# A first stage of v in two passes, with the shift's share of half 0 added later by a matvec

## The chip, the cores and the metric

The kernel runs on one core of a Trainium2 chip. The metric is the device time of one execution in microseconds. It is one launch; everything from the first load to the last store is in it.

## The reference, cut to what matters

One layer of a diffusion backbone over 640 tokens (128 context tokens, 512 sample tokens), model width 2048, all in float32. The part that the change touches is the beginning:

```python
sh1, sc1, g1, sh2, sc2, g2 = modulation(cond, w_mod, b_mod)   # silu(cond) @ w_mod + b_mod, 2 conditions
u = rmsnorm(x, g_pre_mix) * (1.0 + sc1) + sh1
q, k, v, o, ig, fg, z, xbc, dt = split(u @ w_in)              # v: 1024 columns, gates: 48 columns
```

After it come a bidirectional mLSTM with four heads (it uses q, k, v and the gates ig, fg), a bidirectional SSD (it uses xbc after a small convolution, and dt), the output projection, and an MLP. A row of u can be written as x·a1 times the norm of its token plus the shift, where a1 = g_pre_mix (1 + sc1). So a column block of u @ w_in is the norm of the token times (x·a1) @ w_in plus sh1 @ w_in; the last term is one row for each of the two conditions.

## The kernel before, in words

Activations lie with the model dimension on the partitions (KT = 16 slices of 128 rows, `xT`, `ah`, `al`) and the 640 tokens in the free dimension; NT = 5 token tiles of 128. A product of the first stages is made three times in fp32r: each operand is split into a high part and a rest, and hi·hi, hi·lo and lo·hi are accumulated. `split_block` loads one packed weight block of 128x1024 (512 KB) into a `raw` buffer, copies it to `whi` on ACT (L202) and subtracts into `wlo` on DVE (L203). `mm_b` (L231 to L233) makes three matmuls with 512 moving columns for one token tile and one slice; `mm_a` (L215) makes six with 384 or 256 moving columns, weights stationary.

The first stage (the loop over k from L292 on) does this. All of x is loaded; the sum of squares over the 16 slices is made on ACT (L298) and DVE (L300), and `norm_row` (L165, L176) turns it into one factor per token, spread over the partitions, `rb`. `mod1(k)` loads four blocks of `w_mod` (as two transfers of 1024 KB into `m1`, 4 buffers), multiplies them with the conditions in 16 small matmuls of 256 columns whose stationary tile is 128x32 (L319), and gets the scale `a1` and the shift `modT` of slice k by way of a copy, two transposes (L256) and a sum (`sm`, L257). Then u = x·a1·rb (L339), `ah` = u + shift (L340), `al` = the rest (L341). Slice k is multiplied into two banks for the gates (`gps`), and each pair of slices into five banks for half 0 of v (`vps`). Every slice needs its scale and its shift before it can be multiplied.

After the stage: the gates are transposed, and a long chain of small operations on DVE and ACT (L402 to L525) makes the decay factors from them. Half 1 of v is a projection of its own (`proj_b("v", 1)`), then come q and k of head 0, `mlstm(0)`, q and k of head 1, and so on; the convolution tiles 8 and 12 (`conv_tile`) stand ahead of `mlstm(3)`. Each projection takes `mod_step`s along, 96 and later 128 in all, which load one block (`mraw`) and make the rest of the modulation with four small matmuls (L267). PSUM has 8 banks: in the first stage 5 `v`, 2 `g`, 1 `s`; afterwards 5 `mm`, 2 `ms`, 1 `tr`. The tile `fm` (128x640) has 6 buffers for q, k, convolution tiles and short-lived work.

The framework orders the instructions of each engine and of the load queue on SP ahead of time, from its own model of the times; loads are issued in that order as soon as their buffer is free.

## Time and profile before

| | us |
|---|---|
| median of 3 runs (range) | 2903.09 (2900.97 to 2903.12) |
| the profiled execution | 2905.62 |
| its span, first to last instruction | 2903.6 |
| mean granted TensorE clock | 0.995 of full speed |
| TensorE (PE) busy | 2830.6 |

A busy time counts an instruction from its start to its modelled end; the matmuls of a stream overlap, so their pace is read from the starts in the timeline and not from the mean length. An idle time is put down to the wait that ended last.

### The profile page before, as it was taken

How to read it: one execution, taken by the hardware profiler on the slowest of the kernel's cores; microseconds unless marked ns; L12 is line 12 of the kernel's file. 1: busy time of each engine (PE TensorE's matmuls, PEld its weight loads, DVE VectorE, ACT ScalarE, POOL GpSimd, SP SyncE). 2: the span in 40 equal slices, each digit the busy share in tenths (PEclk: the TensorE clock that was granted, in tenths of full speed). 3: DMA queues.
4: the chain of work that ended last, by engine and by line, in shares of the span. 5: the costliest groups of instructions: out<-in, count | busy, mean ns of one | idle time of the engine just before them, and what ended most of it. 6: DMA issues, size and time to landing. Idle time of an engine off the chain costs nothing.

```text
span 2903.6 us, 48371 instructions
## 1 busy us (share of the span) xinstructions
PE 2830.6 (97%) x18868; PEld 2629.6 (91%) x18868; DVE 1945.6 (67%) x3102; ACT 1280.8 (44%) x2307; POOL 439.4 (15%) x466
## 2 busy tenths in 40 slices
PE   6999999999999999999999999999999999999996
PEld 4679997887887888999999999999999999999996
DVE  4463474786756745677777666666776677678977
ACT  3322333334423433554444444444555555555363
POOL 0000000223211000000000000000014444543212
PEclk9999999999999999999999999999999999999998
DMA  9743434545647767555444333333458999897253
GB/s 369 283 138 115 138 128 138 174 160 159 211 140 227 251 229 263 174 182 167 154 158 143 115 113 109 112 111 117 141 146 169 211 211 204 188 203 180 88 207 142
DMA packets 211748, 498.52 MB, mean 172 GB/s; under 512 B 22424, under 2 KB 111768, under 8 KB 211008
## 3 DMA queue, kind: packets, MB, share of 16 engines
q1 hardware_dynamic: 153872, 429.38, 44.3%
q0 software_dynamic: 39792, 45.73, 10.0%
q10 hardware_dynamic: 17856, 20.32, 1.9%
q8 instruction: 148, 2.42, 0.3%
q14 instruction: 80, 0.66, 0.1%
HBM read 405.33 MB, written 44.97 MB: 155 GB/s over the span
## 4 chain that ended last, share of the span: by engine, by line
PE 83%; DVE 6%; DMA 4%; issue 3%; ACT 1%; POOL 1%; ACTq 0%; DVEq 0%; SPq 0%; POOLq 0%
PE mm L810 17%; PE mm L808 17%; PE mm L809 17%; PE mm L215 11%; PE mm L231 3%; PE mm L233 3%; PE mm L232 3%; PE tr L267 3%; DMA raw<-in_w 2%; DVE wlo L936 2%; POOL pc L1217 1%; PE mod L319 1%; PE vps L231 1%; PE vps L232 1%; DMA R<-hd 1%
## 5 line engine op out<-in xcount | busy, mean ns | idle before, releaser
L936 ACT CAST whi<-raw 128x512 fp32r<-128x512 f32 (+1 forms) x659 | 499.0, 766 | 558.3 <-PE mm L809 323.6
L936 DVE TENSOR_TENSOR wlo<-raw,whi 128x512 fp32r<-128x512 f32 (+1 forms) x659 | 578.2, 886 | 240.2 <-ACT whi L936 234.9
L810 PE MATMUL mm<-ah,wlo 128*128 128x320 f32 x1536 | 475.2, 311 | 5.2 <-DVE wlo L936 4.9
L808 PE MATMUL mm<-ah,whi 128*128 128x320 f32 x1536 | 478.4, 312 | 1.2 <-ACT whi L936 1.2
L809 PE MATMUL mm<-al,whi 128*128 128x320 f32 x1536 | 476.2, 310 | 0.0
L202 ACT CAST whi<-raw 128x1024 fp32r<-128x1024 f32 x162 | 169.3, 1047 | 419.1 <-PE mm L233 131.0
L810 PEld LDWEIGHTS mm<-ah,wlo 128*128 128x128 f32 x1536 | 288.1, 188 | 11.5 <-DVE wlo L936 6.3
L1217 POOL DMA_DIRECT2D pc<-ev x275 | 241.2, 905 | 366.3 <-ACT ev L1216 356.1
L808 PEld LDWEIGHTS mm<-ah,whi 128*128 128x128 f32 x1536 | 288.6, 188 | 8.4 <-issue 6.2
L203 DVE TENSOR_TENSOR wlo<-raw,whi 128x1024 fp32r<-128x1024 f32 x162 | 201.8, 1248 | 140.7 <-ACT whi L202 138.6
L809 PEld LDWEIGHTS mm<-al,whi 128*128 128x128 f32 x1536 | 288.7, 188 | 5.5 <-issue 4.9
L215 PE MATMUL mm<-ah,whi 128*128 128x256 f32 (+1 forms) x768 | 189.6, 319 | 0.0
L215 PE MATMUL mm<-al,whi 128*128 128x256 f32 (+1 forms) x768 | 188.8, 318 | 0.0
L215 PE MATMUL mm<-ah,wlo 128*128 128x384 f32 (+1 forms) x768 | 185.8, 316 | 0.0
L231 PE MATMUL mm<-whi,ah 128*128 128x512 f32 x400 | 161.6, 404 | 0.0
L232 PE MATMUL mm<-wlo,ah 128*128 128x512 f32 x400 | 160.0, 400 | 0.0
L233 PE MATMUL mm<-whi,al 128*128 128x512 f32 x400 | 159.4, 399 | 0.0
L808 PE MATMUL mm<-q,whi 128*128 128x320 f32 x512 | 158.0, 309 | 0.0
L810 PE MATMUL mm<-q,wlo 128*128 128x320 f32 x512 | 157.9, 308 | 0.0
L1216 ACT COPY ev<-mm 128x320 f32<-128x320 f32 x275 | 115.9, 425 | 69.7 <-DMA pc<-ev 45.4
L215 PEld LDWEIGHTS mm<-ah,whi 128*128 128x128 f32 x768 | 121.0, 188 | 10.2 <-issue 9.1
L215 PEld LDWEIGHTS mm<-ah,wlo 128*128 128x128 f32 x768 | 120.6, 188 | 6.9 <-issue 5.8
(399 smaller groups left out, 6709.0 us busy)
## 6 DMA issues: line engine op xcount, KB each, us to landing
raw<-in_w SPq DMA_DIRECT2D x460, 512.0 KB, 3.7
mraw<-in_w SPq DMA_DIRECT2D x128, 512.0 KB, 4.2
pc<-ev POOLq DMA_DIRECT2D x275, 160.0 KB, 5.0
m<-in_w SPq DMA_DIRECT2D x32, 1024.0 KB, 6.8
R<-hd SPq DMA_DIRECT2D x32, 640.0 KB, 6.3
xs<-csd SPq DMA_DIRECT2D x40, 256.0 KB, 5.0
hd<-s ACTq DMA_DIRECT2D x62, 160.0 KB, 3.3
hd<-u ACTq DMA_DIRECT2D x62, 160.0 KB, 1.9
```

Source lines behind the costliest of these rows:

```text
L202: S.copy(hi, t)
L203: V.tensor_sub(lo, t, hi)
L215: PE.matmul(ps[h][:, 0:HW[h]], lhsT=w[:, cs_], rhs=a[:, k, HS[h]], start=(k == 0 and i == 0), stop=(k == KT - 1 and i == 2))
L231: PE.matmul(ps[:, :], lhsT=ah[:, k, tok], rhs=hi[:, wc], start=first, stop=False)
L232: PE.matmul(ps[:, :], lhsT=ah[:, k, tok], rhs=lo[:, wc], start=False, stop=False)
L233: PE.matmul(ps[:, :], lhsT=al[:, k, tok], rhs=hi[:, wc], start=False, stop=last)
L808: PE.matmul(ps, lhsT=wh[:, c], rhs=bh[:, k, :], start=(start and k == 0), stop=False)
L809: PE.matmul(ps, lhsT=wh[:, c], rhs=bl[:, k, :], start=False, stop=False)
L810: PE.matmul(ps, lhsT=wl[:, c], rhs=bh[:, k, :], start=False, stop=(stop and k == nk - 1))
L936: newest[:] = S.copy(hi, src), V.tensor_sub(lo, src, hi)
L1216: S.copy(ev, ps)
L1217: G.dma_start(pi[:, j, :], ev, accum_op=OP.add)
```

## The change

- The stage is cut into two passes over the eight pairs p of slices. In pass 0 `mod1(0, p)` makes the scales of two slices at once; `ah` is x·a1 alone, without norm and without shift, and half 0 of v is multiplied from it. The sums of squares are made along the way, x is loaded pair by pair. At the end of the pass the norm of each token is worked out (`rc5`) and half 0 is multiplied by it as it leaves PSUM. In pass 1 `mod1(1, p)` makes the shifts; u, `ah` and `al` are made as before, and half 1 of v is multiplied in the same stage.
- The blocks of `mod1` come as single transfers of 512 KB, into 5 `m1` and the 2 `mraw` buffers (7 blocks; before, 4 buffers of two blocks).
- The gates become a projection of their own after the stage (`proj_a("g", 0)`).
- The shift's part of half 0 (`v0_steps`): the eight blocks of half 0 are loaded again, multiplied with the shifts in 16 small matmuls of 512 columns, summed over partitions by two full ones, and added to the finished half. These steps take the place of the first eight `mod_step`s (`side_step`).
- `proj_b` takes 12 side steps instead of 8. The convolution tiles 8 and 12 move ahead of `mlstm(0)`, so their two `fm` buffers are held through all heads. The half-0 tile of v is allocated from the start.

```diff
-    for k in range(KT):
-        keys += [("m1", k, j) for j in range(4)]
-        if k % 8 == 0:
-            keys.append(("A", "g", 0, k // 8))
-        if k % 2 == 1:
-            keys.append(("B", "v", 0, k // 2))
-    keys += [("B", "v", 1, j) for j in range(8)]
+    for v in range(2):
+        for p in range(KT // 2):
+            keys += [("m1", v, p, j) for j in range(4)]
+            keys.append(("B", "v", v, p))
+    keys += [("A", "g", 0, j) for j in range(2)]
...
+                for _ in range(2 - j % 2):
+                    side_step()
...
+        def side_step():
+            if first:
+                if next(first[0], "end") == "end":
+                    first.pop()
+                else:
+                    return
+            if mod["n"] < MODCAP[0]:
+                mod_step()
...
-            for k in range(KT):
-                if k % 2 == 0:
-                    SY.dma_start(xT[:, k:k + 2, :], A["xT"][:, k * T:(k + 2) * T].rearrange("p (a b) -> p a b", b=T))
-                sq = rb if k == 0 else (wb, wp)[k % 2].tile([P, 1024], F32, tag=("raw", "mraw")[k % 2], name="sq", bufs=2)[:, 0:T]
-                S.activation(sq, xT[:, k, :], AF.Square)
-                if k:
-                    V.tensor_add(rb, rb, sq)
-            for h in range(2):
-                V.tensor_copy(rb[:, HS[h]], norm_row(rb[:, HS[h]], D,
-                                                     lambda: pv.tile([P, 512], F32, tag="g", name="nrm", bufs=2)))
...
+            def load_m1(v, p):
                 r = []
-                for jj in range(2):
-                    w = p0.tile([P, 2, 1024], F32, tag="m1", name="m1", bufs=4)
-                    b0 = BLK["m1", k, 2 * jj]
-                    SY.dma_start(w, A["w"][b0:b0 + 2].rearrange("b p c -> p b c"))
+                for j in range(4):
+                    i = more["m1"] = more.get("m1", -1) + 1
+                    if i % 7 < 2:
+                        w = wp.tile([P, 1024], F32, tag="mraw", name="mraw", bufs=2)
+                    else:
+                        w = p0.tile([P, 1024], F32, tag="m1", name="m1", bufs=5)
+                    SY.dma_start(w, A["w"][BLK["m1", v, p, j]])
                     r.append(w)
...
-            def mod1(k):
-                ws = load_m1(k)
+            def mod1(v, p):
+                ws = load_m1(v, p)
                 ps = pv.tile([P, 512], F32, tag="s", name="mod1", bufs=1)
                 for kk in range(KT):
                     g = kk % 4
                     PE.matmul(ps[32 * g:32 * g + 32, 0:256], lhsT=scT[:, kk, :],
-                              rhs=ws[kk // 8][:, kk // 4 % 2, g * 256:(g + 1) * 256],
+                              rhs=ws[kk // 4][:, g * 256:(g + 1) * 256],
...
+                for i in range(2):
+                    k = 2 * p + i
+                    if v == 0:
+                        V.tensor_scalar(a1[:, k, :], sm[:, i, :], b1[:, k:k + 1], pp("gpre")[:, k:k + 1],
+                                        OP.add, OP.mult)
+                    else:
+                        V.tensor_scalar(modT[:, k, :], sm[:, i, :], pp("bmod")[:, k:k + 1], None, OP.add)
...
+            def v_pair(vps, v, p):
+                vw = split_block(("B", "v", v, p))
+                for kk in range(2):
+                    k = 2 * p + kk
+                    for t in range(NT):
+                        mm_b(vps[t], t, k, vw[0], vw[1], kk, k == 0, k == KT - 1)
...
-            for k in range(1):
-                mod1(k)
-            for k in range(KT):
-                if k + 1 < KT:
-                    mod1(k + 1)
-                u = p0.tile([P, T], F32, tag="u", name="u", bufs=1)
-                for ci, cc in enumerate((slice(0, P), slice(P, T))):
-                    V.scalar_tensor_tensor(u[:, cc], xT[:, k, cc], a1[:, k, ci:ci + 1], rb[:, cc], OP.mult, OP.mult)
-                    S.activation(ah[:, k, cc], u[:, cc], AF.Identity, bias=modT[:, k, ci:ci + 1])
-                    V.scalar_tensor_tensor(al[:, k, cc], u[:, cc], modT[:, k, ci:ci + 1], ah[:, k, cc],
-                                           OP.add, OP.subtract)
-                if k % 8 == 0:
-                    gw = split_block(("A", "g", 0, k // 8))
-                mm_a(gps, k, gw[0], gw[1])
-                if k % 2 == 0:
-                    continue
-                vw = split_block(("B", "v", 0, k // 2))
-                for kk in range(2):
-                    for t in range(NT):
-                        mm_b(vps[t], t, k - 1 + kk, vw[0], vw[1], kk, k - 1 + kk == 0, k - 1 + kk == KT - 1)
+            mod1(0, 0)
+            load_x(0)
+            for p in range(KT // 2):
+                if p + 1 < KT // 2:
+                    load_x(p + 1)
+                    mod1(0, p + 1)
+                else:
+                    mod1(1, 0)
+                for k in (2 * p, 2 * p + 1):
+                    for ci, cc in enumerate(CC):
+                        S.activation(ah[:, k, cc], xT[:, k, cc], AF.Copy, scale=a1[:, k, ci:ci + 1])
+                        V.scalar_tensor_tensor(al[:, k, cc], xT[:, k, cc], a1[:, k, ci:ci + 1], ah[:, k, cc],
+                                               OP.mult, OP.subtract)
+                    sq = rb if k == 0 else p0.tile([P, T], F32, tag="u", name="sq", bufs=1)
+                    S.activation(sq, xT[:, k, :], AF.Square)
+                    if k:
+                        V.tensor_add(rb, rb, sq)
+                if p == KT // 2 - 1:
+                    pt = pv.tile([P, 512], F32, tag="g", name="nrm", bufs=2)
+                    for i in range(NT):
+                        PE.matmul(pt[:, i:i + 1], lhsT=rb[:, i * P:(i + 1) * P], rhs=ones[:, 0:1],
+                                  start=True, stop=True)
+                    V.tensor_scalar(rc5, pt[:, 0:NT], 1.0 / D, EPS, OP.mult, OP.add)
+                    G.tensor_tensor(rc5, rc5, mhalf[:, 0:NT], OP.pow)
+                v_pair(vps, 0, p)
+            for i in range(NT):
+                V.tensor_scalar(rb[:, i * P:(i + 1) * P], ident, rc5[:, i:i + 1], None, OP.mult)
+            for c in CC:
+                pt = pv.tile([P, 512], F32, tag="g", name="nrm", bufs=2)
+                for i in range(c.start, c.stop, P):
+                    PE.matmul(pt[:, i - c.start:i - c.start + P], lhsT=ones, rhs=rb[:, i:i + P], start=True, stop=True)
+                S.copy(rb[:, c], pt[:, 0:c.stop - c.start])
+            for t in range(NT):
+                if t % 2:
+                    V.tensor_scalar(v_out(vts[0], t), two_heads(vps[t]), rc5[:, t:t + 1], None, OP.mult)
+                else:
+                    S.activation(v_out(vts[0], t), two_heads(vps[t]), AF.Copy, scale=rc5[:, t:t + 1])
+            vps = [pv.tile([P, 512], F32, tag="v", name="vps", bufs=5) for _ in range(NT)]
+            for p in range(KT // 2):
+                if p + 1 < KT // 2:
+                    mod1(1, p + 1)
+                for k in (2 * p, 2 * p + 1):
+                    u = p0.tile([P, T], F32, tag="u", name="u", bufs=1)
+                    for ci, cc in enumerate(CC):
+                        V.scalar_tensor_tensor(u[:, cc], xT[:, k, cc], a1[:, k, ci:ci + 1], rb[:, cc], OP.mult, OP.mult)
+                        S.activation(ah[:, k, cc], u[:, cc], AF.Identity, bias=modT[:, k, ci:ci + 1])
+                        V.scalar_tensor_tensor(al[:, k, cc], u[:, cc], modT[:, k, ci:ci + 1], ah[:, k, cc],
+                                               OP.add, OP.subtract)
+                v_pair(vps, 1, p)
...
+        vts.append(v_new(vq1.enter_context(tc.tile_pool(name="vq1", bufs=1, reuse_waits="tile"))))
+        for t in range(NT):
+            (V.tensor_copy if t % 2 else S.copy)(v_out(vts[1], t), two_heads(vps[t]))
...
+        shT = gp.tile([P, KT, 32], F32, name="shT")
+        V.memset(shT, 0.0)
+        V.tensor_copy(shT[:, :, 0:2], modT[:, 0:KT, :])
+        vpart = gp.tile([P, 512], F32, name="vpart")
+        vcol = gp.tile([P, 2], F32, name="vcol")
+        V.reduce_sum(vcol, ident.rearrange("p (g b) -> p b g", g=4)[:, 0:2, :], axis=mybir.AxisListType.X)
+        def v0_steps():
+            w = []
+            for j in range(8):
+                w.append(raw_block(("B", "v", 0, j), "mraw"))
+                if j % 2:
+                    ps = trt()
+                    for g in range(4):
+                        k = 2 * j - 2 + g
+                        PE.matmul(ps[32 * g:32 * g + 32, :], lhsT=shT[:, k, :],
+                                  rhs=w[k // 2][:, k % 2 * 512:(k % 2 + 1) * 512], start=True, stop=True)
+                    if j == 1:
+                        V.tensor_copy(vpart, ps)
+                    else:
+                        V.tensor_add(vpart, vpart, ps)
+                if j < 7:
+                    yield
+            for c in range(2):
+                sel = gp.tile([P, P], F32, tag="vsel", name="vsel", bufs=2)
+                V.tensor_scalar(sel, ones, vcol[:, c:c + 1], None, OP.mult)
+                ps = trt()
+                PE.matmul(ps, lhsT=sel, rhs=vpart, start=True, stop=True)
+                for t in range(NT):
+                    if (t > 0) == c:
+                        V.tensor_add(v_out(vts[0], t), v_out(vts[0], t), two_heads(ps))
+        first[:] = [v0_steps()]
+        gT = fmt()[0:48, :]
+        for i, ps in enumerate(proj_a("g", 0)):
+            S.copy(gT[:, HS[i]], ps[0:48, 0:HW[i]])
...
-        vts.append(v_tile(proj_b("v", 1)))
         qk0 = qk(0)
+        pre = {}
+        for m in (8, 12):
+            pre[m] = fmt()
+            conv_tile(m, pre[m])
...
-        pre = {}
-        for m in (8, 12,):
-            pre[m] = fmt()
-            conv_tile(m, pre[m])
```

## Rows read from the trace of the kernel before

**Rows 1.** The page: PE in part 1, and one group of part 5 (busy us, mean ns).
```profile
PE 2830.6 (97%) x18868; PEld 2629.6 (91%) x18868; DVE 1945.6 (67%) x3102; ACT 1280.8 (44%) x2307; POOL 439.4 (15%) x466
...
L202 ACT CAST whi<-raw 128x1024 fp32r<-128x1024 f32 x162 | 169.3, 1047 | 419.1 <-PE mm L233 131.0
```

**Rows 2.** Busy time in five stretches: PE, PEld, DVE, ACT, POOL, clock, DMA share, GB/s.
```profile
0.00:22.89 22.89, 0.00 (x1) 0.00 (x1) 13.74 (x24) 12.41 (x18) 1.20 (x8) 1.00 0.90 344
22.89:39.88 16.99, 15.10 (x101) 9.16 (x102) 8.66 (x24) 4.66 (x8) 1.57 (x2) 1.00 1.03 409
39.88:146.50 106.62, 103.21 (x801) 70.89 (x799) 48.94 (x119) 31.17 (x55) 1.46 (x2) 1.00 0.82 305
...
148.72:213.38 64.66, 64.66 (x335) 48.73 (x332) 45.05 (x119) 14.28 (x28) 2.17 (x3) 1.00 0.46 153
```

**Rows 3.** What PE waited for in the first 500 us: total, times, longest.
```profile
PE nrm L165 <- DVE rb L300: 22.9, 1, 22.9
PE mod L319 <- DVE sm L257: 3.3, 9, 1.0
PE gps L215 <- ACT ah L340: 1.2, 3, 0.8
```

**Rows 4.** Timeline of ACT at the start: start, length, line, operation, tiles.
```profile
7.55 0.74 ACT L298 ACTIVATE rb<-xT 128x640 f32<-128x640 f32 x1 [4.04 <-DMA xT<-in_xT]
...
18.72 1.36 ACT L298 ACTIVATE sq<-xT 128x640 f32<-128x640 f32 x2 [0.22 <-DMA xT<-in_xT]
```

**Rows 5.** PE's groups in the first 39.9 us: busy, mean ns, idle before.
```profile
L319 PE MATMUL mod<-m,scT 128*32 128x256 f32 x64 | 6.9, 508 | 0.4 <-DVE sm L257 0.4
L176 PE MATMUL nrm<-rb,ones 128*128 128x128 f32 x10 | 3.3, 448 | 0.0
...
L256 PE MATMUL mod1t<-ident,part 128*128 128x128 f32 x4 | 0.8, 273 | 0.0
```

**Rows 6.** Timeline of PE in one period of the first stage.
```profile
107.50 1.93 PE L319 MATMUL mod<-m,scT 128*32 128x256 f32 x32 [0.27 <-DVE sm L257]
109.36 0.50 PE L231 MATMUL vps<-whi,ah 128*128 128x512 f32 x1
...
112.54 0.46 PE L215 MATMUL gps<-al,whi 128*128 128x384 f32 x2
112.83 0.45 PE L215 MATMUL gps<-ah,wlo 128*128 128x384 f32 x2
...
114.14 1.07 PE L319 MATMUL mod<-m,scT 128*32 128x256 f32 x16
115.14 0.50 PE L231 MATMUL vps<-whi,ah 128*128 128x512 f32 x1
...
121.44 0.85 PE L319 MATMUL mod<-m,scT 128*32 128x256 f32 x12 [0.27 <-DVE sm L257]
```

**Rows 7.** Timeline of PE in the second half of v.
```profile
149.06 0.40 PE L232 MATMUL mm<-wlo,ah 128*128 128x512 f32 x1
...
155.48 0.40 PE L233 MATMUL mm<-whi,al 128*128 128x512 f32 x1
155.81 0.64 PE L267 MATMUL tr<-mraw,scT 128*32 128x256 f32 x8
156.38 0.50 PE L231 MATMUL mm<-whi,ah 128*128 128x512 f32 x1
```

**Rows 8.** Chain of waits, 221 to 275 us: start, length, what.
```profile
221.79 7.08 PE mm L215 x48
...
256.62 0.43 PE ms L595 x2
```

**Rows 9.** Timeline of ACT: first and last step of the gate chain.
```profile
146.45 0.73 ACT L402 COPY fm<-gps 48x384 f32<-48x384 f32 x2
...
202.31 0.24 ACT L507 ACTIVATE gu<-gu 128x40 f32<-128x40 f32 x1 [0.25 <-DVE gu L504]
```

**Rows 10.** DVE's costliest group, 290 to 440 us.
```profile
L565 DVE SCALAR_TENSOR_TENSOR fm<-cv,cw,fm 128x512 f32<-128x512 f32 x24 | 18.4, 768 | 0.2
```

More of the change, by code (lines that the diff above doesn't have):

```diff
@@ L287, in build, with v_new, v_out, two_heads @@
         V.tensor_scalar(b1, pp("bmod")[:, 16:32], 1.0, None, OP.add)
+        vq = ExitStack()
+        vp = vq.enter_context(tc.tile_pool(name="vq", bufs=1, side="right", reuse_waits="tile"))
+        vq1 = ExitStack()
+        rc5 = cp.tile([P, NT], F32, name="rc5")
+        def v_new(pool):
+            vt = pool.tile([P, NT, 2, 257], F32, tag="v", name="v", bufs=1)
+            V.memset(vt[:, :, :, 256:257], 1.0)
+            return vt
+        def v_out(vt, t):
+            return vt[:, t, :, 0:256]
+        def two_heads(ps):
+            return ps.rearrange("p (h e) -> p h e", h=2)
+        vts = [v_new(vp)]
         pctx = ExitStack()
@@ L326, in mod1 @@
                 mod_sum(sm, part, pv.tile([P, 512], F32, tag="s", name="mod1t", bufs=1))
-                V.tensor_scalar(a1[:, k, :], sm[:, 0, :], b1[:, k:k + 1], pp("gpre")[:, k:k + 1], OP.add, OP.mult)
-                V.tensor_scalar(modT[:, k, :], sm[:, 1, :], pp("bmod")[:, k:k + 1], None, OP.add)
-            vps = [pv.tile([P, 512], F32, tag="v", name="vps", bufs=5) for _ in range(NT)]
-            gps = [pv.tile([P, 512], F32, tag="g", name="gps", bufs=2) for _ in range(2)]
-            for k in range(1):
-                mod1(k)
@@ new lines, in load_x @@
+            def load_x(p):
+                SY.dma_start(xT[:, 2 * p:2 * p + 2, :],
+                             A["xT"][:, 2 * p * T:(2 * p + 2) * T].rearrange("p (a b) -> p a b", b=T))
+            def v_pair(vps, v, p):
[4 more added lines that the diff above has]
+                        mm_b(vps[t], t, k, vw[0], vw[1], kk, k == 0, k == KT - 1)
+            CC = (slice(0, P), slice(P, T))
```

25 lines of the change are left out of this document (5 added, 20 removed).

## The prediction

> **What bounds the kernel now.** The page comes first: PE is busy for 2830.6 of 2903.6 us [rows 1], so the kernel goes as fast as PE's queue, and the question is where PE stands still near the change. The table of stretches shows it. Until 22.89 us PE does nothing at all. From there to 39.88 us it has only small work. From 39.88 to 146.5 us the first stage runs, 103.2 of 106.6 us busy, while the loads run at 305 GB/s; and from 148.72 to 213.38 us PE is busy all the time with half 1 of v and what goes along with it [rows 2]. The waits say why: PE waited 22.9 us for the sum of squares, and in the rest of the first 500 us only a few, 3.3 of them because one small product of the modulation stands in PE's queue right behind the sum of the one before [rows 3]. So the first stage is not short of data after its start. It is filled by PE, and the prize lies in the first 40 us.
>
> How much of that start is idle? The work done by 39.88 us is two `mod1` (64 instructions [rows 5], 1.86 us for each run of 32 [rows 6]: 3.7 us), the norm (3.3 us), four transposes (0.8 us) [rows 5], four pairs of gate matmuls at 0.29 us [rows 6] and six of v at 0.23 us (2.5 us together). That is 10.3 us, so 29.6 us are idle.
>
> One period of the full stage, from one run of 32 small matmuls to the next like it, takes 13.94 us [rows 6] and covers two slices. In it are 30 matmuls of v at 0.229 us (28 of them in 6.42 us [rows 7]): 6.87 us; the run of 32, 1.86 us, and two of 16 at 1.00 us; six gate pairs at 0.29 us, 1.74 us [rows 6]; and two pairs of transposes at 0.38 us or less (a pair is 0.8/2 [rows 5]). The sum is 13.2 us, and 0.7 us are left for the wait on the sum and for changes between the small and the large stationary tile.
>
> **The change, step by step.** I build the new stage from these paces up to the point where v, the gates and the matvec are done.
>
> *Start.* x lands in pairs of slices of 655 KB, the first at 7.55 us, the eighth at 18.72 us: 1.60 us each, 410 GB/s [rows 4]. Loads come in the order of the code: four blocks of 524 KB for `mod1(0, 0)`, two pairs of x, four blocks for `mod1(0, 1)`, the first block of v. That is 6.03 MB; less the 0.66 MB that had landed at 7.55 us, at 410 GB/s, the block of v is there at 20.6 us. The copy into `whi` takes 1.05 us [rows 1], so the first matmul of v starts at 21.7 us; both `mod1`, `ah` and `al` of the first slice fit ahead of it. Bounds: the block of v goes ahead of the second four (2.1 MB or 5.1 us earlier, 16.6 us), or the other six pairs of x go ahead of it (6 x 1.6 us later, 31 us).
>
> *The two passes.* 16 blocks of v x 30 matmuls x 0.229 us = 109.9 us; 14 more `mod1` at 1.86 us and 14 pairs of transposes at 0.38 us, 31.4 us; the norm, 3.3 us as before. The wait on the sum goes, since 6.9 us of v now lie between two `mod1`; for tile changes I leave 0.35 us for each block, 5.6 us. DMA does not bind: a block of pass 0 needs 3.28 MB, 8.0 us at 410 GB/s, against 9.4 us of PE; pass 1 needs 2.62 MB. DVE, busy 48.9 of 106.6 us [rows 2], has 6.4 us of work in a period; with an eighth of what it did ahead of the stage (13.7 us) added, the sums of squares, it is 8.1 us, still under 9.4, and ACT has less.
>
> *Pieces.* A `mod1` whose blocks come one by one may be cut up in PE's order. Cut in two it costs 2.00 in place of 1.86 us [rows 6]; a run of 8 alone costs 0.57 us and 0.10 us at its front [rows 7], so four of them 2.7 us. Before, half of them were cut in two; I take 1 us in all, bounds 0 (none cut) and 11 us (all cut in four).
>
> *Change of pass.* The norm is spread by matmuls after the last block of pass 0, then u and `ah` of the first slice follow, and five banks must be emptied first (on two engines). `mod1(1, 1)`, 2.2 us, covers most of it: I take 1 us, bounds 0 and 5.
>
> So v ends at 21.7 + 109.9 + 31.4 + 3.3 + 5.6 + 1 + 1 = 173.9 us. Nothing is added for emptying the banks at the end, since the first bank is done before the last and gates need two.
>
> *Gates.* They leave the stage (48 pairs x 0.29 = 13.9 us, already not counted above) and become a projection of 96 matmuls: two runs of 48 at 7.08 us [rows 8], 14.2 us, in the open. *Matvec.* It is new work on a full PE, hidden by nothing: four groups like a `mod_step` but with twice the columns, 4 x (2 x 0.57 + 0.10) = 5.0 us [rows 7], and two full fp32 matmuls of 512 columns at twice the 0.43 us of 257 columns [rows 8], 1.7 us. Bounds 5.0 and 6.7 us; nothing suggests less than the pace of rows for small tiles, so 6.7. The eight blocks loaded again (4.2 MB) meet a DMA that moves 153 GB/s there [rows 2] and cost nothing.
>
> That gives 173.9 + 14.2 + 6.7 = 194.8 us. Before, the same point is 148.72 + 240 x 0.229 = 203.7 us, less 1.0 us of later work done between 146.5 and 148.72 us: 202.7. (The other 9.7 us up to 213.38 are `mod_step`s and products of the gate chain, which come after in the new order and cost the same there; slots for `mod_step` ahead of the output projection are 90 instead of 88.) The difference is -7.9 us.
>
> *Gate chain.* It ran from 146.45 to 202.55 us, 56.1 us [rows 9], under half 1 of v and part of q. Now it begins after the gates' projection, under q and k of head 0 (28.3 us), two convolution tiles (28.3 us), most of the matvec and its own products: some 66 us. That just covers it. But the convolutions' taps, eight of 0.77 us for each tile [rows 10], 12.3 us for both and an estimated 17 with their smaller operations, and the adds of the matvec, an estimated 4 us, share DVE with it: up to 77 us, 11 us too long, unless q and k of head 1 are drawn ahead (another 28.3 us). I take 1.3 us, bounds 0 and 26 (below). Holding two `fm` buffers longer leaves four for q and k, two heads, and costs nothing as long as a head's chain fits under the next head's projections.
>
> Sum: -6.6 us. On the profiled execution's 2905.6 us this is 2899.0; the median lies 2.5 us below that execution, so I predict **2896.5 us**, 0.23% faster. A measurement of this kernel tells about 0.2%, 5.8 us, from no change.
>
> **Rivals.**
>
> *No change that can be measured.* The start comes later or the small products are cut up. With six pairs of x ahead, +9.5 us, the sum is +3: 2906. With half of the `mod1` cut in four, +5.5, it is -1: 2902. For it: loads are issued as soon as a buffer is free, and x's tile has no buffer to wait for. Against it: SP's order follows the code as far as buffers allow.
>
> *Slower: the gate chain shows.* If PE's order is fixed with `mlstm(0)` ahead of head 1's projections, as the code has it, each us by which the chain outlasts its 66 us of cover is lost. The chain at 77 us costs 11 us, and the head's own start adds to it: before, q and k of head 0 were done near 241.7 us (four runs of 7.08 us from 213.38), and the first product of the state came at 256.62 us [rows 2, 8], 15 us later, with other projections between. It decides from 12.4 us of stall on; with 15 us the time is 2910, with all 26 us 2921. Against it: PE waited only a few us outside the start in 500 us [rows 3], so the order written ahead does draw other matmuls into such gaps.
>
> *Slower: smaller loads.* If single transfers of 512 KB run slower than pairs, pass 0 becomes bound by them. At the 305 GB/s of the full stage before [rows 2], taken as a limit, a block of pass 0 takes 10.8 in place of 9.4 us, 8 x 1.4 = 11 us: 2908. Against it: pairs of x of 640 KB landed at 410 GB/s with several on their way [rows 4]. This is a rule of the Trainium skill, "DMA: Bandwidth & Descriptors", section "Bandwidth": to batch transfers to 1 MiB or more for at least 75% of the peak. By its section "Anatomy of one DMA" (2.0 us and bytes over 436 GB/s) one such block would take an estimated 3.2 us, 164 GB/s if each had to wait for the one before, and both passes would be bound by loads, some 100 us more. The trace disagrees for a queue of transfers: 640 KB every 1.6 us.
>
> **How the numbers follow.** The forecast with its gain kept (start at 16 to 22 us, few pieces, chain covered) 0.47, giving 2887 to 2897; no change by start or pieces 0.33; slower by the gate chain 0.16, by smaller loads 0.04. Hence faster 0.47, same 0.33, slower 0.20. The range goes from all lower bounds (start -5, pieces -1, matvec -1.7, chain -1.3: 2887.5, taken as 2887) to the gate chain at 15 us, 2910; the rest of that case lies outside.
>
> **What would show it.** In the changed kernel's trace: the first matmul of v near 21.7 us; PE nearly full from there on; the last of half 1 of v near 174 us; the gates' two runs of some 7.1 us right behind; no new wait of PE on DVE or ACT ahead of the first state product of `mlstm(0)`. The prediction is wrong if the starts of v's blocks stand more than 9.4 us apart (loads or pieces), if PE waits for x or a block of v beyond 25 us, or if `mlstm(0)` finds PE idle.

## The result, and the profile after

The changed kernel takes 2946.86 us (median of 4 runs, 2941.19 to 2949.20) against 2902.12 us for the kernel before beside it (2900.97 to 2903.12): a ratio of 1.0152, 95% interval 1.0137 to 1.0167, 44 us slower. The forecast was 2896.5 us. The profiled execution takes 2945.27 us, its span 2943.3 us, at a mean granted clock of 0.986.

The page after (part 1), in answer to [rows 1]: PE is still busy 97% of the span. The share that said "PE sets the pace" before says the same of a kernel that is 44 us slower.

```profile
PE 2864.3 (97%) x18904; PEld 2646.2 (90%) x18904; DVE 1971.3 (67%) x3145; ACT 1297.0 (44%) x2341; POOL 436.5 (15%) x465
```

The first stage itself came as forecast. Timeline of PE after, at the first matmul of v, at the end of half 1 and at one group of the matvec:

```profile
21.57 1.43 PE L228 MATMUL vps<-whi,ah 128*128 128x512 f32 x5 [0.51 <-ACT whi L200]
...
175.37 1.33 PE L230 MATMUL vps<-whi,al 128*128 128x512 f32 x5
176.54 0.35 PE L213 MATMUL mm<-ah,whi 128*128 128x384 f32 x1
...
184.62 1.07 PE L481 MATMUL tr<-mraw,shT 128*32 128x512 f32 x8
185.61 0.57 PE L213 MATMUL mm<-ah,whi 128*128 128x384 f32 x2
```

The first matmul of v starts at 21.57 us (forecast 21.7), half 1 ends at 176.5 us (173.9), and one of the four groups of the matvec (x8 in the row) takes 0.99 us of PE's queue (1.24). What PE waited for in the first 500 us after (total, times, longest), in answer to [rows 3]: the 22.9 us for the sum of squares are now 4.0; 10.0 us of waits for blocks of the modulation are new, all of them ahead of the first matmul of v (7.0 us are the wait for the very first block).

```profile
PE mod L340 <- DMA mraw<-in_w: 7.2, 2, 7.0
PE nrm L389 <- DVE rb L385: 4.0, 1, 4.0
PE mod L340 <- DMA m<-in_w: 2.8, 4, 2.2
```

One thing in the stage was not forecast: the granted clock of TensorE. Busy time after, just ahead of a stretch at the lower of the clock's two levels and in it (PE, PEld, DVE, ACT, POOL, clock, DMA share, GB/s):

```profile
36.00:43.90 7.90, 4.88 (x49) 2.13 (x47) 5.61 (x11) 4.70 (x9) 0.00 (x0) 1.00 1.02 409
43.90:50.70 6.80, 5.11 (x23) 3.83 (x23) 4.34 (x10) 2.62 (x3) 1.18 (x1) 0.50 1.03 408
```

The 4.0 us of the sum of squares end at 45.59 us. After a stretch in which PE was busy 4.88 of 7.90 us, its clock was 0.50 for 6.8 us. Half of the 5.11 us that PE was busy there, an estimated 2.6 us, is lost by it. Every version of the changed kernel below has such a 6.8 us stretch, beginning between 43 and 49 us; the profile of the kernel before shows none up to 1315 us.

Then the loss. Busy time in stretches after (PE, PEld, DVE, ACT, POOL, clock, DMA share, GB/s):

```profile
0.00:21.57 21.57, 9.74 (x68) 2.16 (x68) 6.62 (x23) 7.82 (x13) 1.21 (x8) 1.00 0.90 339
21.57:176.50 154.93, 150.22 (x976) 108.02 (x977) 90.91 (x186) 62.75 (x111) 2.64 (x3) 0.98 0.74 282
...
240.00:480.00 240.00, 239.79 (x1487) 214.62 (x1486) 131.65 (x348) 79.59 (x188) 21.16 (x23) 1.00 0.36 119
480.00:560.00 80.00, 73.73 (x466) 62.99 (x465) 52.89 (x127) 24.57 (x56) 14.30 (x16) 0.96 0.54 178
...
940.00:960.00 20.00, 17.65 (x105) 12.74 (x104) 13.09 (x33) 9.59 (x25) 7.58 (x8) 0.97 0.63 178
960.00:980.00 20.00, 14.20 (x82) 8.31 (x85) 12.58 (x30) 5.63 (x12) 2.73 (x3) 0.61 0.91 319
980.00:1000.00 20.00, 15.77 (x109) 10.75 (x102) 15.87 (x34) 9.26 (x19) 0.66 (x2) 0.74 0.68 219
```

Before, PE was busy 78.22 us between 480 and 560 us (x489) and 99.77 us between 900 and 1000 us (x620); after, it issued 466 and 492 matmuls there. From 952 us on the z projection is used up while the SSD's end is still to come (before, z ends at 958.2 us and the SSD's last product with `xs` stands at 906.5), PE turns sparse, and the granted clock averages 0.61 and 0.74.

How much of the loss is standing still, and how much the clock? Up to point D of the table below (columns as above; first the kernel before, then the changed one, then the sum over the changed kernel's seven stretches at the lower level, 43.9 to 992.8 us):

```profile
0.00:1119.67 1119.67, 1087.01 (x7070) 907.65 (x7071) 683.40 (x1483) 377.45 (x751) 130.70 (x146) 1.00 0.57 191
...
0.00:1156.00 1156.00, 1116.40 (x7090) 920.30 (x7091) 704.58 (x1524) 390.57 (x784) 126.92 (x145) 0.98 0.55 188
...
sum 44.40, PE 36.76 PEld 25.33 DVE 28.39 ACT 13.08 POOL 5.95; mean PE 5.25 PEld 3.62 DVE 4.06 ACT 1.87 POOL 0.85
```

The changed kernel comes to D 36.3 us later. PE stood still for 39.6 us against 32.7, only 6.9 us more. For 36.8 us it was busy at the lower level, and half of that, an estimated 18.4 us, is time lost to the clock. The remaining 11.0 us were not taken apart; the matvec is in them, and matmuls that come ahead of D in one kernel and behind it in the other. So half of the loss up to D hides in PE's busy time; the busy share of 97% cannot show it.

The gates' chain and the first head, on ACT after, in answer to [rows 9]: its first copy at 193.6 us (before 146.5), its last steps at 250.5 us (before 202.3), the first k weighted with `wk` at 264.45 us (before 248.75).

```profile
193.63 0.73 ACT L501 COPY fm<-mm 48x384 f32<-48x384 f32 x2
...
250.51 0.22 ACT L603 ACTIVATE wk<-wk 128x40 f32<-128x40 f32 x1
...
264.45 0.65 ACT L689 ACTIVATE kw<-ms,wk 128x128 f32<-128x128 f32 x2
```

Four points of the middle of the kernel, each the start of an instruction in its profiled execution, serve for all that follows: A the first state product of `mlstm(0)`, B the first state product of the SSD, C the SSD's last product with `xs`, D the first product of the norm behind the output projection. The last column is the ratio to the kernel before timed beside it.

| kernel | A | B | C | D | ratio |
|---|---|---|---|---|---|
| before | 256.5 | 520.7 | 906.5 | 1119.7 | |
| after | 271.4 | 517.8 | 969.6 | 1156.0 | 1.0152 |
| a_conv_late | 261.1 | 524.8 | 960.8 | 1152.6 | 1.0085 |
| a_one_side | 271.2 | 517.7 | 920.6 | 1120.3 | 1.0094 |
| a_both | 260.0 | 524.8 | 899.4 | 1116.8 | 1.0050 |
| a_no_matvec | 255.0 | 518.8 | 910.7 | 1118.8 | 1.0001 |
| a_chain_short | 242.1 | 510.2 | 901.2 | 1120.0 | 1.0009 |
| b_two_side | 256.6 | 520.9 | 951.8 | 1148.2 | 1.0071 |
| b_side_load | 256.8 | 521.1 | 910.8 | 1131.5 | 1.0034 |
| b_side_pe | 256.9 | 521.1 | 948.8 | 1139.5 | 1.0055 |
| b_conv_early | 283.7 | 535.6 | 916.4 | 1138.5 | 1.0050 |
| b_chain_late | 270.4 | 532.9 | 916.8 | 1138.6 | 1.0047 |
| b_less_v | 240.6 | 504.9 | 890.0 | 1103.2 | 0.9938 |

### The profile page after: what moved, and what is told of

Read it like the earlier page. It is cut to its first block, busy times and chain, and to the rows that moved or that the text cites. A ratio compares the mean times of both kernels' runs of the same rounds, so it can differ in the third digit from the quotient of the medians.

```text
span 2943.3 us, 48611 instructions
## 1 busy us (share of the span) xinstructions
PE 2864.3 (97%) x18904; PEld 2646.2 (90%) x18904; DVE 1971.3 (67%) x3145; ACT 1297.0 (44%) x2341; POOL 436.5 (15%) x465
## 3 DMA queue, kind: packets, MB, share of 16 engines
q8 instruction: 148, 2.42, 0.3%
## 4 chain that ended last, share of the span: by engine, by line
PE 90%; DVE 4%; DMA 4%; issue 1%; ACT 1%; SPq 0%; POOL 0%; DVEq 0%; ACTq 0%; POOLq 0%
PE mm L903 20%; PE mm L905 20%; PE mm L904 20%; PE mm L213 10%; PE mm L228 3%; PE mm L229 3%; PE mm L230 2%; PE tr L264 2%; PE vps L228 1%; PE vps L229 1%; PE vps L230 1%; PE mod L340 1%; DMA ohb<-hsp 1%; DMA mraw<-in_w 1%; DVE wlo L1031 1%
## 5 line engine op out<-in xcount | busy, mean ns | idle before, releaser
L903 PEld LDWEIGHTS mm<-ah,whi 128*128 128x128 f32 x1536 | 289.8, 189 | 12.4 <-issue 9.1
L905 PEld LDWEIGHTS mm<-ah,wlo 128*128 128x128 f32 x1536 | 289.4, 189 | 9.1 <-DVE wlo L1031 4.5
L201 DVE TENSOR_TENSOR wlo<-raw,whi 128x1024 fp32r<-128x1024 f32 x162 | 202.7, 1253 | 138.5 <-ACT whi L200 138.1
L904 PEld LDWEIGHTS mm<-al,whi 128*128 128x128 f32 x1536 | 289.8, 189 | 4.1 <-issue 3.7
L213 PE MATMUL mm<-ah,whi 128*128 128x384 f32 (+1 forms) x800 | 199.8, 321 | 0.7 <-DVE v L456 0.7
L213 PE MATMUL mm<-al,whi 128*128 128x384 f32 (+1 forms) x800 | 200.1, 321 | 0.0
L213 PE MATMUL mm<-ah,wlo 128*128 128x384 f32 (+1 forms) x800 | 196.7, 318 | 0.0
L213 PEld LDWEIGHTS mm<-ah,whi 128*128 128x128 f32 x800 | 127.7, 190 | 12.5 <-issue 10.2
L213 PEld LDWEIGHTS mm<-al,whi 128*128 128x128 f32 x800 | 128.2, 190 | 8.3 <-issue 7.1
L213 PEld LDWEIGHTS mm<-ah,wlo 128*128 128x128 f32 x800 | 127.4, 190 | 3.9 <-issue 2.9
L229 PE MATMUL mm<-wlo,ah 128*128 128x512 f32 x320 | 129.9, 406 | 0.0
L228 PE MATMUL mm<-whi,ah 128*128 128x512 f32 x320 | 129.6, 405 | 0.0
```

The lines of the kernel that those rows point to most:

```text
L201: V.tensor_sub(lo, t, hi)
L213: PE.matmul(ps[h][:, 0:HW[h]], lhsT=w[:, cs_], rhs=a[:, k, HS[h]], start=(k == 0 and i == 0), stop=(k == KT - 1 and i == 2))
L228: PE.matmul(ps[:, :], lhsT=ah[:, k, tok], rhs=hi[:, wc], start=first, stop=False)
L229: PE.matmul(ps[:, :], lhsT=ah[:, k, tok], rhs=lo[:, wc], start=False, stop=False)
L903: PE.matmul(ps, lhsT=wh[:, c], rhs=bh[:, k, :], start=(start and k == 0), stop=False)
L904: PE.matmul(ps, lhsT=wh[:, c], rhs=bl[:, k, :], start=False, stop=False)
```

## The experiments

The rival causes at the start: the pieces that the change moves beside its idea (tiles, side steps), which took cover (matmuls that PE can do while a chain of small dependent steps runs) away from the chains of the heads and the SSD; the work that it adds (the matvec, with the steps that it displaces); the later gates.

A kernel whose name begins with a is the changed one with an edit, with b the kernel before with an edit. 0.1% is 2.9 us; the difference between two ratios is good to some 0.2%.

**Undoing the moves.** Two parts of the change move work that is not the stage: tiles 8 and 12, and twelve side steps for eight. Each is undone alone, then both.

```diff
 # a_conv_late: the tiles go back ahead of mlstm(3), the matvec is finished behind qk(0)
-        pre = {}
-        for m in (8, 12):
-            pre[m] = fmt()
-            conv_tile(m, pre[m])
+        for _ in first[0]:
+            pass
 # a_one_side: proj_b
-                for _ in range(2 - j % 2):
-                    side_step()
+                side_step()
 # a_both: the two together
```

> Theory A (matmuls that fill run out: half 1 of v no longer stands beside the gate chain, and the two convolution tiles are used up ahead of head 0, so the projections are gone when mlstm(3), the SSD and the turn of the mLSTM output still need cover): with the tiles 8 and 12 back ahead of mlstm(3), most of the loss comes back, 2900 to 2920. Theory B (twelve side steps for each projection of o and z hold up the SSD): no gain from this alone, 2935 to 2950.

> The changed kernel with one side step for each block of o and z again, as before the change. Theory A: within 10 us of the changed kernel, 2937 to 2957. Theory B: 2900 to 2920, and PE no longer stands still between 950 and 992 us.

> The changed kernel with both put back: tiles 8 and 12 ahead of mlstm(3) and one side step for each block. Theory A: as with the tiles alone, 2900 to 2920. Theory B: as with the side steps alone, 2900 to 2920. If neither explains it, it stays over 2930, and what is left is the two-pass stage with the gates and the matvec behind it.

Measured: 1.0085 (1.0066 to 1.0104), 1.0094 (1.0077 to 1.0112), 1.0050 (1.0034 to 1.0066). From 1.0152 the tiles give back 0.44 to 0.67%, the side steps 0.35 to 0.58%, by the order in which they are undone. Neither undone alone comes back to the 2900 to 2920 us that its theory expected (2933.65 and 2935.74 us): both moves cost. With twelve side steps C stands at 960 to 970 us, with eight at 899 to 921: the side steps hold up the SSD. The tiles set A. But a_both, which leads the kernel before by 2.9 us at D, loses it in a new place. Busy time in a_both, columns as above: a part of the modulation is missing and its blocks are loaded and multiplied in one go, with nothing beside them (eight steps between 1215 and 1262 us).

```profile
1220.00:1240.00 20.00, 18.68 (x147) 14.92 (x145) 8.58 (x26) 1.75 (x4) 0.85 (x1) 1.00 0.41 135
1240.00:1260.00 20.00, 12.85 (x53) 8.17 (x54) 15.97 (x16) 7.73 (x7) 0.00 (x0) 0.66 0.70 247
```

**Each move alone on the kernel before.**

```diff
 # b_conv_early: ahead of mlstm(0) in place of mlstm(3)
+        pre = {}
+        for m in (8, 12):
+            pre[m] = fmt()
+            conv_tile(m, pre[m])
 # b_two_side: proj_b
-                if mod["n"] < MODCAP[0]:
-                    mod_step()
+                for _ in range(1 if name == "v" else 2 - j % 2):
+                    if mod["n"] < MODCAP[0]:
+                        mod_step()
```

> The kernel before the change with only the tiles 8 and 12 moved ahead of mlstm(0). Theory A: slower than before by 5 to 25 us, since the same cover is missing at mlstm(3). Theory B: the same as before within 6 us.

> The kernel before the change with twelve side steps instead of eight in each projection of o and z (half 1 of v keeps eight). Theory B (the steps packed into o and z hold up the SSD and use up the cover of its end): slower than before by 8 to 20 us. Theory C (they cost only where the cover is already short, in the changed kernel): the same within 6 us.

Measured: 1.0050 (1.0033 to 1.0068) and 1.0071 (1.0056 to 1.0086). Neither adds an operation; both cost. In b_two_side everything is in place up to B, C comes 45 us late, and PE goes sparse behind it:

```profile
940.00:960.00 20.00, 20.00 (x113) 14.66 (x111) 9.39 (x22) 6.03 (x11) 2.74 (x3) 1.00 0.61 212
960.00:980.00 20.00, 12.30 (x79) 5.96 (x76) 12.86 (x25) 5.88 (x10) 0.00 (x0) 0.61 0.87 288
```

**Which half of a side step it is.** On the kernel before, loads without products, and products without loads.

```diff
 # b_side_load: one more block in every even step of o and z
+                    if name != "v" and j % 2 == 0:
+                        raw_block(("m", mod["n"] // 4, mod["n"] % 4), "mraw")
 # b_side_pe: every second step of an even j takes its columns from a resident tile
+            w = raw_block(("m", p, j), "mraw") if load else None
...
+                          rhs=w[:, g * 256:(g + 1) * 256] if load else scT...[:, 0:256],
```

> The kernel before, with 16 more loads: every even block of the o and z projections loads one more block of 512 KB into an mraw buffer, and nothing reads it; no step of the modulation is moved. 12 side steps in o and z cost some 20 us on the kernel before (2927.15 against 2907.45). Theory L: what holds up the SSD there is the load, a buffer of mraw and a place in the load queue ahead of the SSD's own loads. Then this kernel stands at 2920 to 2927. Theory P: it is the place of a step's four small products and its add in the queues of TensorE and VectorE and in the one tr bank. Then the loads alone cost little: 2905 to 2912.

> The kernel before with 12 side steps in o and z, as in b_two_side, but each additional step loads nothing: its four products take their moving columns from a resident tile (this leaves out that part of the modulation, in some 13 steps). Theory L (load, mraw buffer): close to the kernel before, 2905 to 2912. Theory P (products, adds, tr bank): as with the loads, 2922 to 2930. A value in the middle of both kernels says that the costs add.

Measured: 1.0034 (1.0021 to 1.0047) and 1.0055 (1.0040 to 1.0070), in us 10 and 16. Neither theory has it alone, but they act in different places: with the products C is 42 us late (948.8), with the loads alone 4 us (910.8), and those lose the rest up to D. The delay of the SSD is that of the products, sums and the `tr` bank; which of the three was not taken apart.

**The matvec, and where its displaced steps go.** a_no_matvec is a_both without the matvec (the shift's part of half 0 of v is left out); the other three are a_both with the missing steps of the modulation in other places.

```diff
 # a_no_matvec
-        first[:] = [v0_steps()]
 # a_conv_steps: proj_a, ahead of the matmuls of a block
+                if name == "x" and j == 0:
+                    side_step()
 # a_steps_in_stage: one mod_step for each pair in pass 1, in the g banks; mraw not used for m1 there
+                mod_step(lambda: pv.tile([P, 512], F32, tag="g", name="modg", bufs=2))
 # a_qk_steps: proj_a
+                for _ in range(2 if name in ("q", "k") and j == 0 else 1):
+                    side_step()
```

> As the run with both put back (2923), without the matvec: the shift's part of half 0 of v is left out, and the first eight side steps are modulation steps again. Theory D: 5.7 us of work less and eight of the missing steps done in time, 2905 to 2914. If the loss was in the stage itself, it stays near 2917.

> The changed kernel with the tiles 8 and 12 ahead of mlstm(3), one side step for each block of o and z, and three instead of two side steps in each convolution projection. Theory D (what is left of the loss in the run with both put back is that 14 steps too few were done by the output projection, and PE waits for them near 1250 us): the wait near 1250 us is gone and the time is 2900 to 2912 beside 2907 of the kernel before. Against it: if the steps in the convolutions hold up the SSD as those in o and z did, 2915 or more.

> As the run with both put back, with one modulation step in each of the eight blocks of pass 1, in the banks that the gates had; pass 1 then has five buffers for its blocks. Theory D: 82 slots and the early steps again, 2903 to 2914. If the loads of pass 1 do not keep up with five buffers, PE waits in the stage and it is 2920 or more.

> The kernel with one side step for each block and tiles 8 and 12 late (a_both, 2922.94), and one more side step in the first block of each q and k projection, ahead of the SSD: the eight displaced steps are made before 500 us. Theory D (each displaced step costs only where it is made in bulk or holds up the SSD): the wait of 11 to 16 us at 1240 us goes and nothing comes for it but the steps' own time that was always there, 2908 to 2912. Theory X (what is gained ahead of the heads is given back in the SSD's stretch, whatever the steps do): 2917 to 2923, like the kernel with steps in the first stage (2920.15).

Measured: 1.0001 (0.9991 to 1.0011), 1.0158 (1.0143 to 1.0173), 1.0039 (1.0024 to 1.0054), 1.0034 (1.0022 to 1.0046). The matvec and the eight steps that it displaces cost 0.49% together as a_both has them, 14 us. Steps in the convolutions repeat the mistake of the side steps: C at 985.5 us. Steps in the stage or in q and k remove the bulk wait at 1240 us (PE is busy there all the time), but the gain, 3 and 5 us, is smaller than that wait and hardly clear of the error, so theory D's ranges are missed (2920.15 and 2915.10 us): C and D come later (926.5 and 1133.7; 913.2 and 1127.2 us). Some 10 us stay as the price of the matvec with its displaced steps.

**Is time saved ahead of the heads kept?** a_no_matvec has the stage's gain, none of the moves, and still only equals the kernel before. So I took work away from the kernel before, in half 1 of v:

```diff
+            if full:   # False in proj_b("v", 1) alone
                 PE.matmul(ps[:, :], lhsT=ah[:, k, tok], rhs=lo[:, wc], start=False, stop=False)
```

> The kernel before with the second of three products left out in half 1 of v (80 matmuls of 0.229 us, 18.3 us of TensorE's work between 149 and 213 us; the product of the high activations with the rest of the weights is left out there). The chain of the gates keeps its place. Theory K: time saved ahead of the heads is kept to the end, since TensorE is full behind: 18 us less, about 2889. Theory X: the stretch from the first state product to the end of the SSD gives most of it back, because its chains are only just covered: the end comes 0 to 8 us earlier, 2899 to 2907, with idle time of TensorE growing by 10 to 18 us between 250 and 1000 us.

Measured: 0.9938 (0.9921 to 0.9954), 17.7 us less for 18.3 us of matmuls; A, B, C and D are all 15.8 to 16.5 us earlier. Theory K holds there, X falls.

**The gates' chain.** One thing that a_no_matvec has otherwise than b_less_v is a late chain (another is the stretch at the lower clock in its stage). Its timeline on ACT: the first weighted k comes 0.3 us behind `wk`, so the chain sets the start of `mlstm(0)`, at 248.05 us where before it came at 248.75 us without having to wait for `wk`.

```profile
196.86 0.73 ACT L499 COPY fm<-mm 48x384 f32<-48x384 f32 x2
...
247.78 0.24 ACT L601 ACTIVATE wk<-wk 128x40 f32<-128x40 f32 x1 [2.74 <-DVE wk L598]
247.92 0.22 ACT L603 ACTIVATE dec<-dec 128x40 f32<-128x40 f32 x1
248.05 0.37 ACT L683 ACTIVATE kw<-ms,wk 128x128 f32<-128x128 f32 x1
```

```diff
 # b_gates_late: the gates leave the stage, as in the change
-                mm_a(gps, k, gw[0], gw[1])
...
+        vts.append(v_tile(proj_b("v", 1)))
+        for i, ps in enumerate(proj_a("g", 0)):
 # b_chain_late: the stage as it was, the chain also reads half 1 of v, which is written ahead of it
+        vts.append(v_tile(proj_b("v", 1)))
+        V.scalar_tensor_tensor(gt, vts[1][:, :, 0, 0:48], 0.0, gt, OP.mult, OP.add)
 # a_gates_in (from a_qk_steps) and a_gates_in_nm (from a_no_matvec): in pass 1, ahead of v_pair
+                    mm_a(gps, k, gw[0], gw[1])
 # a_chain_short (from a_no_matvec) and b_chain_short
-        for st in (1, 2, 4, 8, 16, 32, 64):
+        for st in (1,):
```

> The kernel before with one thing of the change: the gates leave the first stage and become a projection behind half 1 of v. TensorE's work is the same (13.9 us taken out of the stage, 14.2 us put behind half 1). Only the chain of the gates starts later: its first copy at 200 to 213 us in place of 146.5, and with some 51 us of length it ends at 251 to 264 us, where before the first weighted k (the copy with wk) of mlstm(0) stood at 248.8 us without having to wait for it. Theory G (the start of mlstm(0) sets the time, though TensorE never stands still for it): first weighted k at 252 to 265 us, total 5 to 16 us above the kernel before, 2911 to 2922. Theory W (TensorE's queue alone sets the time; what waits is replaced by other matmuls at no cost): within 4 us of the kernel before.

> The kernel before, its first stage untouched, with one false dependence: the third operation of the gates' chain also reads half 1 of v (times zero), so the chain goes on at some 212 us in place of 149, 60 us later; one small operation of VectorE is added and nothing else. Theory G (the start of mlstm(0) sets the time though TensorE finds other matmuls meanwhile): first weighted k at 262 to 268 in place of 248.8 us, total 10 to 18 us above the kernel before, with no single wait of TensorE that would account for it. Theory W (TensorE's queue alone sets the time): within 4 us of the kernel before, and the excess of the kernel with late gates (16.3 us) came from its first stage, which lost the gates' matmuls as filler.

Measured: 1.0058 (1.0036 to 1.0080) and 1.0047 (1.0032 to 1.0061). b_gates_late moved A by 22.6 us to 279.1 (its first weighted k comes at 272.1 us, later than forecast), but its stage also lost some us without the gates' matmuls in it, so it is no clean test (PE's waits from 40 to 150 us sum to 9.8 us there, to 4.4 before). b_chain_late is nearer to one: its stage is untouched, though the projection of half 1 stands earlier in the code too. Its chain ends at 260.5 us, A is 13.9 us late, the time 13.6 us longer. PE hardly waited there; its wait list from 200 to 480 us has one row, and from 480 to 1000 us nine small ones (total, times, longest; the largest three). They sum to 9.7 us, where the four of the kernel before sum to 3.3:

```profile
PE ms L503 <- DVE fm L495: 1.5, 1, 1.5
...
PE tr L267 <- DVE macc L273: 2.5, 2, 2.2
PE ms L729 <- POOL xs L726: 2.2, 2, 1.2
PE tr L666 <- DVE fm L571: 1.2, 1, 1.2
```

PE drew other projections ahead while the head was not ready, and some of the time stands in those small waits on DVE and POOL from 480 us on (6.4 us more than before, of 13.6). The rest has no row in the list. What the waits show of the loss stands far from the cause.

> The whole computation: the kernel with displaced steps in q and k and tiles 8 and 12 late (a_qk_steps, 2915.1), with the gates accumulated in pass 1. Theory G: the first weighted k moves from 250.6 to some 240 us and the total by as much, 2903 to 2907; the matvec and its adds to half 0 (5.7 us of matmuls) stand ahead of mlstm(0) and keep it from more. Theory W: 2913 to 2917.

> The kernel with tiles 8 and 12 late, one side step for each block and no matvec (a_no_matvec, 2908.75; the shift's part of half 0 of v is left out), with the gates accumulated in pass 1, in the two free banks, slice by slice ahead of v's matmuls of the same pair. TensorE's work is the same, v ends some 14 us later, the chain of the gates starts some 21 us earlier: 175 in place of 196.9 us. Theory G: first weighted k at 234 to 240 in place of 248.1 us, total 8 to 14 us less, 2895 to 2901, and with it below the kernel before. Theory W: no change, 2907 to 2911.

> The changed kernel with tiles 8 and 12 late, one side step for each block and no matvec (a_no_matvec, 2908.75), with six of the seven doubling steps of the running maximum left out (12 operations of 0.81 us in the chain of the gates; this leaves out most of the running maximum, beside the shift's part of half 0). Theory G: the chain ends 9.7 us earlier, first weighted k at 238 to 239 in place of 248.1 us, and the total falls by as much, 2897 to 2901, under the kernel before. Theory W: within 4 us of 2908.75, 2905 to 2911.

> The control for it: the kernel before with the same six steps left out. There the chain ended at 201.7 us and the first weighted k came at 248.8 us, so both theories expect no change, within 4 us of the kernel before; less than that would say that these operations cost VectorE's time elsewhere.

Measured: 1.0025 (1.0014 to 1.0036), 1.0039 (1.0025 to 1.0053), 1.0009 (1.0000 to 1.0019), 0.9995 (0.9986 to 1.0005). The first two are misses: the gates' last matmuls were put at the end of pass 1 all the same, the chain began at 190 to 192 us and not at 175, and a_gates_in_nm came out slower than a_no_matvec (C at 900.5, D at 1123.3 us). a_chain_short settles more: there the chain ends at 231.9 us, A comes at 242.1 us, 14.4 us ahead of the kernel before, as early as in b_less_v. That lead is 10.5 us at B, 5.3 us at C and gone at D. So theory G holds in one direction only: a late chain costs, an early one brings nothing to the changed kernel (its 2909.46 us lie in theory W's range). No version of the changed kernel beats the kernel before; the best that computes everything is a_gates_in at 1.0025.

## Why the prediction was wrong

The stage was right, within 3 us: start 21.57 for 21.7 us, end of v 176.5 for 173.9, the gates' projection and a matvec group of about a microsecond behind it. The 2.6 us that are missing are what the lower clock costs there by the estimate above; the sum had no term for the clock. PE stood still for 29.3 us up to 176.5 us before and for 16.5 us after (21.57 and 7.68 against 11.83 and 4.71 us), 12.7 us less. The prediction's 29.6 us of idle time by 39.88 us were too many: PE was busy 15.10 us in its own [rows 2], so 24.8 us were idle, since the small products took longer there (6.9 us for 64 in [rows 5]) than at the full stage's pace. The forecast of the new stage does not rest on that figure. That loads of 512 KB would bind, the rival, did not happen: PE was busy for 150.2 of 154.9 us of the two passes and waited for no block of the modulation in them, and the loads ran at 409 GB/s from 36 to 43.9 us. The rule of the Trainium skill ("DMA: Bandwidth & Descriptors", section "Bandwidth") to batch transfers to 1 MiB or more decides nothing here; the trace does not agree that single blocks of 512 KB cost this stage its pace. What that section of the Trainium skill measured are loads issued by GpSimd; the loads here are issued by SP.

**The step that failed** is the one that carried 194.8 against 202.7 us through to the end. It held that what lies behind that point "come after in the new order and cost the same there", and that holding two `fm` buffers longer "costs nothing as long as a head's chain fits". PE's 97% made moved matmuls look free to place. They were not. For the side steps the traces show why: the products of o and z that cover the SSD's chain are used up before its end, PE waits, and the clock falls. For the tiles they show the late first head and small waits behind it; that the lost cover is the cause there is argued. By the runs, the 44 us and the stage's own gain divide into

- tiles 8 and 12 ahead of `mlstm(0)`: 0.44 to 0.67% in the changed kernel, 0.50% alone on the kernel before; forecast 0. They delay the first head, since their matmuls stand ahead of it (A 271.4 against 260.0 us in a_both);
- twelve side steps for eight in o and z: 0.35 to 0.58%, alone 0.71%; forecast 0. C comes 49 to 61 us later with them, and z is used up before the SSD's end;
- the matvec with the steps it displaces: 0.49% in a_both, about 0.33% at its best place; forecast 6.7 us (0.23%) for the matvec and nothing for the steps. The matmuls were sized well (four groups at 0.99 us and two full products); the eight displaced steps were counted as places (90 for 88, by way of o and z) and not priced;
- the gain of the stage: the 12.7 us of idle time are saved at 176.5 us, but with the moves and the matvec undone (a_no_matvec, 1.0001) the end comes no earlier. New waits and the lower clock, both forecast at nothing, take it (rows below).

**The gate chain** was among the rivals and priced at 1.3 us, bounds 0 and 26. Its price as shown by b_chain_late (13.6 us for a chain that ends at 260.5 us) lies within the bounds, and in a_no_matvec it took the stage's lead at A, which came back when the chain was shortened; the sign that I named for it, a new wait of PE ahead of the first state product, did not come (in b_chain_late it is the one wait of 1.5 us). That sign was wrong: in a queue that is filled from other projections the delay does not show as a wait there.

**Where the stage's gain went.** Busy time up to A and from A to D (columns as above) in the kernel before, then in a_no_matvec, then the sum over the two stretches of a_no_matvec at the lower clock up to D (48.5 to 55.4 and 758.5 to 761.9 us):

```profile
0.00:256.46 256.46, 227.21 (x1556) 169.88 (x1557) 130.65 (x308) 75.62 (x133) 7.85 (x17) 1.00 0.67 244
256.46:1119.67 863.21, 859.80 (x5515) 737.77 (x5515) 552.75 (x1175) 301.83 (x620) 122.85 (x129) 1.00 0.54 176
...
0.00:255.00 255.00, 237.07 (x1571) 181.31 (x1572) 145.13 (x328) 89.96 (x166) 6.72 (x14) 0.99 0.64 233
255.00:1118.80 863.80, 855.00 (x5451) 731.68 (x5450) 547.98 (x1181) 299.99 (x618) 131.97 (x131) 1.00 0.55 176
...
sum 10.30, PE 10.12 PEld 8.18 DVE 7.04 ACT 3.25 POOL 2.71; mean PE 5.06 PEld 4.09 DVE 3.52 ACT 1.63 POOL 1.35
```

Ahead of A, PE stands still 11.3 us less than before. From A to D it stands still 5.4 us more, and the lower clock takes an estimated 5.1 us (half of 10.12). That leaves 0.8 us, and D comes 0.9 us earlier. This is an account of one execution of each, and some 50 records of matmuls fewer stand ahead of D in a_no_matvec, so it says where time went and is no proof of a cause.

**What stays open.** Why PE waits more between B and D in the changed kernel without matvec and moves: the list of PE's waits from 480 to 1000 us has 8.9 us in a_no_matvec and 9.2 us in a_chain_short, most of it on small products behind DVE and POOL, against 3.3 us before. In a_chain_short these waits and one more stretch at the lower clock (764.2 to 767.7 us) explain about 8 of the 14.4 us of its lead at A; the rest has no row. The order of instructions was written ahead by the framework and is another one; that this is the cause is only argued. How much the order can do is seen in a_gates_in_nm, the same matmuls in another order: 10.2 us ahead of a_no_matvec at C, 4.5 us behind it at D.

## What to carry to other kernels

A busy share of 97% says which engine sets the time, not that its work may be moved about: before placing a moved or displaced piece at no cost, find the latency chains that it covers now and count what is left to cover them at their end. Mark the start of each chain (here A to D) in both traces; a delay that fills itself from later work may show no wait where it arises and is paid where that work runs out. Compare the time at the lower clock as well as the idle time. And undo the side moves of a change one by one before judging its idea: here they were two thirds of the loss.

## What had not been expected of the hardware

The clock makes a gap in cover dearer. In the changed kernel z is used up at 952 us and PE waits for small chains and loads. From 958.6 to 972.3 us and from 982.5 to 992.8 us the granted clock was 0.50, the lower of its two levels (1.2 and 2.4 GHz). The eight records of a modulation step took 0.64 us ahead of such a stretch and 1.08 us in it:

```profile
957.14 0.64 PE L264 MATMUL tr<-mraw,scT 128*32 128x256 f32 x8
...
962.35 1.08 PE L264 MATMUL tr<-mraw,scT 128*32 128x256 f32 x8 [1.56 <-DMA mraw<-in_w]
```

In the stage, five matmuls of v took 2.42 us at 0.50 (47.74 to 50.16 us), 0.48 us each, and 0.23 us each at 1.00 from 53 us on. From 1000 to 1020 us the clock was back at 1.00. a_both shows the same around its bulk of modulation steps (0.66 on average from 1240 to 1260 us), and b_two_side from 960 to 980 us (0.61). A group of four small fp32 products (x8 in the rows) took 0.99 us with 512 moving columns and 0.57 us with 256 [rows 7]: 1.7 times the time for twice the columns.
